# Rows that land last first, and blocks asked for one group ahead, for the unsplit experts of a mixture layer

## The chip, the cores and the metric

The kernel runs on one core of one Trainium2 chip. The metric is the device time of one execution in microseconds (us), lower is better.

## What is computed

The reference runs a small model of two blocks over 256 tokens of width 1024: two hybrid layers (mLSTM and dilated attention), a pooling layer with a dense feed-forward part, and an attention layer with a mixture of experts behind it. The change touches the mixture alone:

```python
def moe_ffn(x, router, w_gu, w_down):
    xt = x.reshape(B * S, D)                       # 256 x 1024
    logits = (xt @ router).astype(jnp.float32)
    top_v, top_i = lax.top_k(logits, TOP_K)        # 2 of 8 experts
    w = jax.nn.softmax(top_v, axis=-1)
    combine = ...                                  # weight of each expert for each token
    for e in range(N_EXPERTS):                     # 8, d_ff 3584
        y = y + combine[:, e:e + 1] * swiglu(xt, w_gu[e], w_down[e])
```

Everything is float32. Each expert has 42 MiB of weights, so all eight are 336 MiB, and each of them is read once.

## The kernel before

The experts are sorted by the number of tokens that chose them, and place 0 has most. Places 0 to 3 are the **split** experts: tiles of 128 token rows (place 0 has a second one of 64). Each MiB of their weights lands in a buffer of the tag `raw` and is split into a high and a low part (`whi` by ScalarE in line 147, `wlo` by VectorE in line 148). A product is then three matmuls of 128x512 (lines 209 to 211), or two for the tile of 64 rows (lines 1304 and 1305). I call these the wide products. Places 4 to 7 are the **unsplit** experts (`full` in the code): tiles of 64 rows (places 4 and 5) or 32 rows (6 and 7). Their products read `raw` as it landed, in plain float32, with 64 or 32 columns of the array, in line 1313. I call these the narrow products. The trace shows each of them as two MATMUL records.

Each expert is worked through in seven steps of 512 hidden units. One step has three **blocks** of 2 MiB: gate (`up1`), up (`up2`) and, two steps later, down (`down`). A block is two DMAs of 1 MiB on SyncE's queue (line 132, `wload`), the first for the rows k = 0 to 3 (0 and 1 for down), the second for the rest. The **group** of a block is all its products for one tile: eight narrow products for an unsplit expert, in the order of k.

`run_experts` is a generator that stops after each group. `moe_layer` runs two of them: places 0 to 3 in the outer loop, and places 6, 7, 4, 5 as `light`, which is moved on by a share of a group for each group of the outer one (`due` grows by 1.5 with place 0, by 0.86 with places 1 to 3). All eight of them share `K.raw`, seven buffers of 1 MiB. A wide block is asked for by `ahead` after the products of the block before it in the same generator. An unsplit block is asked for in `take`, at the head of its own group. A load waits until one of the seven buffers is free, with all later loads queued behind it. A buffer is free when `whi` and `wlo` are made (split), or when the last narrow product has read it (unsplit).

The order of instructions on each engine is made when the kernel is built: a scheduler takes the program's order and its own estimate of the times, and may set other work of the engine between two products of a group when it believes that the second half has not landed. On the chip each engine keeps that order.

Of the kernel before, what the change touches and what calls it, by code (L numbers as in the profile page):

```python
# [18 lines left out]
KT = D // 128  # L19
# [132 lines left out]
def behind(K, hold=None):  # L152

    es = ExitStack()
    for ins in K.hold if hold is None else hold:
        es.enter_context(K.tc.issue_after(ins.ins))
    return es


class Raw:  # L160


    def __init__(self, K, src, kt, n):
        self.per = min(kt, 2048 // n)
        self.parts = [wload(K, src[:, k:k + self.per, :], self.per, n) for k in range(0, kt, self.per)]
# [48 lines left out]
def bank(K, tag):  # L214
    return K.ps.tile([128, 512], F32, name=tag, tag=tag, bufs=K.banks[tag])
# [255 lines left out]
def gate_rows(K, pool, cst, gT, S):  # L471
# [9 lines left out]
    nc.gpsimd.memset(one, 1.0)  # L481
    LI, LF, FC, G, EN, TMP, TMP2, M = range(8)
    R = lambda q: gm if q == M else (ga if q < 4 else gb)[:36, q % 4, :]
# [9 lines left out]
    for d in range(2):  # L493
        s = slice(32 * d, 32 * d + 4)
        v = (lambda a: a[s]) if d == 0 else (lambda a: a[s][:, ::-1])
        nc.vector.tensor_tensor_scan(v(R(FC)), v(one), v(R(LF)), 0.0, op0=OP.mult, op1=OP.add)
    nc.vector.tensor_tensor(R(G), R(LI), R(FC), op=OP.subtract)
    for d in range(2):
        s = slice(32 * d, 32 * d + 4)
        v = (lambda a: a[s]) if d == 0 else (lambda a: a[s][:, ::-1])  # L500
        nc.vector.tensor_tensor_scan(v(R(M)), v(one), v(R(G)), -BIG, op0=OP.mult, op1=OP.max)
    nc.vector.tensor_tensor(R(TMP), R(FC), R(M), op=OP.add)
# [3 lines left out]
    pt = bank(K, "acc")[:, :144].rearrange("p (q t c) -> p q t c", q=2, t=2)  # L506
    for q, src in enumerate((G, EN)):
        for t in range(2):
# [729 lines left out]
def buffer(K, pool, name, i, shape, dt, bufs):  # L1238

    b = K.boxes.get(name)  # L1240
    return b[i % len(b)] if b else pool.tile(shape, dt, name=name, bufs=bufs)
# [17 lines left out]
def gather(K, pool, x, R, cw, p, tl, n):  # L1259

    gather_x(K, pool, x, R, p, tl, n)
    gather_w(K, pool, cw, p, tl, n)
# [37 lines left out]
def prod(K, tl, ps, x, w, start, stop):  # L1300

    nc = K.nc
    if tl.kind == "h":
        nc.tensor.matmul(ps, x[:, 0, :], w[0], start=start, stop=False)
        nc.tensor.matmul(ps, x[:, 0, :], w[1], start=False, stop=stop)
    else:
        mm3(nc, ps, (x[:, 0, :], x[:, 1, :]), w, start, stop)


def prod_full(K, tl, ps, c, x, w, start, stop):  # L1310


    K.nc.tensor.matmul(ps[tl.m * c:tl.m * c + tl.m], x, w, start=start, stop=stop)


def fold(K, pool, a, ps, m=64):

    K.nc.scalar.activation(a, ps[64:128, :], AF.Copy)
    K.nc.vector.tensor_tensor(a, ps[0:64, :], a, op=OP.add)
    if m == 32:  # L1320
        b = pool.tile([32, 512], F32, name="fq")
        K.nc.scalar.activation(b, a[32:64], AF.Copy)
        K.nc.vector.tensor_tensor(a[0:32], a[0:32], b, op=OP.add)
    return a[:m]


class Expert:
    def __init__(self, p, tiles):
        self.p, self.tiles = p, [Tile(*t) for t in tiles]
        self.full = self.tiles[0].full  # L1330


def run_experts(K, pool, A, x, R, ri, cw, y, experts, hook=None, last=False):
# [3 lines left out]
    NF = FE // 512  # L1337

    def begin(E):
        with behind(K, K.line):  # L1340
            e = nc.sync.value_load(ri[0:1, E.p:E.p + 1], min_val=0, max_val=NE - 1)
        gu = A["moe_gu"][ds(e, 1)].rearrange("o c q p (k n) -> (o c) q p k n", k=4)
        E.gu = [Packed(gu[c], 4) for c in range(2 * NF)]
        E.dn = Packed(A["moe_dn"][ds(e, 1)].rearrange("o b p (k n) -> (o b) p k n", k=2), 2)
        for n, tl in enumerate(E.tiles):
            tl.n, tl.g = (f"l{E.p}", "l") if tl.full else (n, n)
        enter(E, 0)

    def enter(E, n):
        if E.tiles[n].xg is None:  # L1350
            gather(K, pool, x, R, cw, E.p, E.tiles[n], E.tiles[n].n)

    def load(kind, E, f):
        B = Raw if E.full else W
        return B(K, E.gu[f + NF * kind], KT, 512) if kind < 2 else B(K, E.dn[:, f * 4:f * 4 + 4, :], 4, 1024)

    def take(kind, E, f):
        got.append((kind, E, f))
        if (kind, E, f) not in blocks:
            blocks[kind, E, f] = load(kind, E, f)  # L1360
        return blocks.pop((kind, E, f))

    def ahead():
# [3 lines left out]
        if n < len(order) and not order[n][1].full:  # L1367
            blocks[order[n]] = load(*order[n])

    def up1(E, f):  # L1370
        w = take(0, E, f)
        for tl in E.tiles:
            ps = bank(K, "mm")
            for k in range(KT):
                if tl.full:
                    G = 128 // tl.m
                    prod_full(K, tl, ps, k % G, tl.xg[:, k], w(k, 0, 512), k < G, k >= KT - G)
                else:
                    prod(K, tl, ps, tl.xg[:, k], w(k, 0, 512), k == 0, k == KT - 1)
            a = buffer(K, pool, f"sg{tl.g}", E.p * NF + f, [128, 512], F32, 2)  # L1380
            nc.scalar.activation(a[:tl.m], fold(K, pool, a[:64], ps, tl.m) if tl.m < 128 else ps, AF.Silu)
            tl.sg[f] = a

    def up2(E, f):
        w = take(1, E, f)
        for tl in E.tiles:
            ps = bank(K, "mm")
            for k in range(KT):
                if tl.full:
                    G = 128 // tl.m  # L1390
                    prod_full(K, tl, ps, k % G, tl.xg[:, k], w(k, 0, 512), k < G, k >= KT - G)
                else:
                    prod(K, tl, ps, tl.xg[:, k], w(k, 0, 512), k == 0, k == KT - 1)
            m = tl.m
            u = ps if m == 128 else fold(K, pool, pool.tile([64, 512], F32, name="fu"), ps, m)
            nc.vector.tensor_tensor(tl.sg[f][:m], u, tl.sg[f][:m], op=OP.mult)
# [17 lines left out]

    def down(E, f):
        w = take(2, E, f)
        for tl in E.tiles:
            if tl.full:
                if f == 0:
                    tl.acc = [bank(K, "acc") for _ in range(2)]  # L1420
                for k in range(4):
                    for h in range(2):
                        if tl.m == 32:
                            prod_full(K, tl, tl.acc[h], 2 * (k % 2) + (h ^ (k // 2)), tl.hT[f][:, k],
                                      w(k, h * 512, (h + 1) * 512), f == 0, f == NF - 1)
                        else:
                            prod_full(K, tl, tl.acc[h], h ^ (k % 2), tl.hT[f][:, k],
                                      w(k, h * 512, (h + 1) * 512), f == 0 and k < 2, f == NF - 1 and k >= 2)
                continue
            if tl.sb:  # L1430
                if f == 0:
                    a = buffer(K, pool, "sacc", 0, [128, D], F32, 1)
                    tl.acc = [a[:, 0:512], a[:, 512:1024]]
                for h in range(2):
                    ps = bank(K, "mm")
                    for k in range(4):
                        prod(K, tl, ps, tl.hT[f][:, k], w(k, h * 512, (h + 1) * 512), k == 0, k == 3)
                    if f == 0:
                        nc.vector.tensor_copy(tl.acc[h], ps)
                    else:  # L1440
                        nc.vector.tensor_tensor(tl.acc[h], ps, tl.acc[h], op=OP.add)
                continue
            if f == 0:
                tl.acc = [bank(K, "acc") for _ in range(2)]
            for k in range(4):
                for h in range(2):
                    prod(K, tl, tl.acc[h], tl.hT[f][:, k], w(k, h * 512, (h + 1) * 512),
                         f == 0 and k == 0, f == NF - 1 and k == 3)
# [35 lines left out]
    def settle():  # L1484
# [3 lines left out]
        if late:  # L1488
# [3 lines left out]
    late, begun, blocks, got = [], set(), {}, []  # L1492
    N = len(steps)
    order = [(kind, *steps[i - (kind == 2) * 2]) for i in range(N + 2) for kind in range(3)
             if (i < N if kind < 2 else i >= 2 and not (last and i == N + 1))]
    for i in range(N + 2):
        for E, f in steps[i:i + 3]:
            if id(E) not in begun:
                begun.add(id(E))
                begin(E)  # L1500
        if i < N:
            E, f = steps[i]
# [15 lines left out]
        if i >= 2:  # L1518
            E, f = steps[i - 2]
# [15 lines left out]
def moe_layer(K, x, A, out, ps1, S):  # L1535
    nc = K.nc
    with ExitStack() as es:
# [6 lines left out]
        with K.tc.tile_pool(name="exp", reuse_waits="tile", bufs=1) as ep:  # L1544
# [15 lines left out]
            for t in range(2):  # L1560
                nc.vector.tensor_scalar(y[:, t, :], x[:, t, :], ALPHA, None, op0=OP.mult)
            go = lambda *a: run_experts(K, ep, A, x, R, ri, cw, y, *a)
            E[0].tiles[1].sb = True
            b = [ep.tile([128, 2048], t, name=f"box{n}") for n, t in enumerate((F32R, F32, F32))]
# [170 lines left out]
```

## Time and profile before

| | us |
|---|---|
| median of three runs | 2013.59 |
| lowest and highest | 2011.82, 2013.74 |
| the profiled execution, its own time | 2013.14 |
| span of its trace | 2011.4 |
| start of the first expert DMA | 1083.3 |
| end of the mixture's products on TensorE | about 1995 |

The profiled execution stands 0.45 us under the median, and 1.7 us lie outside its span. TensorE is busy for 96% of the span. From 1083 us on the mixture's weights stream in, and the DMA engines are as busy as TensorE. An end of a matmul in the trace is modelled, so for TensorE I read the distances from start to start.

### The profile page before, as it was taken

Reading aid. Unit: us, or ns where it says so; the run is one execution under the profiler, and the core shown is the slowest. Engines: PE = TensorE matmul, PEld = TensorE weight load, DVE = VectorE, ACT = ScalarE, POOL = GpSimd, SP = SyncE. Lnnn points to the kernel's source line nnn. Section 1 sums busy time; section 2 is a strip of 40 time slices with the busy share of each in tenths; the row PEclk is TensorE's granted clock in tenths of the full one; section 3 lists DMA queues with packets and bytes.
Section 4 is the critical chain, followed back from the end, with each engine's and each line's share of the span. In section 5 each row is a group of like instructions: output and inputs, shape, how many; then the busy total and the mean of one; then the engine's idle time right before and its main releaser. Section 6 shows DMA issues by size and latency. Waiting matters only on the chain. (4 is left out here: it accounts for less than half of the span.)

```text
span 2011.4 us, 27838 instructions
## 1 busy us (share of the span) xinstructions
PE 1936.6 (96%) x11039; PEld 1492.6 (74%) x11039; DVE 1263.4 (63%) x1721; ACT 960.5 (48%) x1195; POOL 35.2 (2%) x39
## 2 busy tenths in 40 slices
PE   7999999999999899999997999999999999999996
PEld 7879998888999899989776766665556556655563
DVE  6876555877555644466767555666666665656655
ACT  6565444665444444435342544445455544545442
POOL 0000000000000200000000000000000000000000
PEclk9999999999999999999997999999999999999998
DMA  9434555535555365552004789999999999999994
GB/s 341 164 116 160 176 190 179 173 126 171 203 173 205 138 200 186 166 191 85 6 1 180 303 348 391 391 403 380 426 405 413 409 395 422 399 410 384 420 422 168
DMA packets 137851, 523.68 MB, mean 260 GB/s; under 512 B 12016, under 2 KB 44144, under 8 KB 94832
## 3 DMA queue, kind: packets, MB, share of 16 engines
q1 hardware_dynamic: 137568, 521.74, 67.5%
q8 instruction: 89, 1.46, 0.3%
q14 instruction: 50, 0.41, 0.1%
q10 hardware_dynamic: 144, 0.07, 0.0%
HBM read 520.73 MB, written 1.05 MB: 259 GB/s over the span
## 5 line engine op out<-in xcount | busy, mean ns | idle before, releaser
L148 DVE TENSOR_TENSOR wlo<-raw,whi 128x2048 fp32r<-128x2048 f32 (+2 forms) x335 | 716.0, 2155 | 328.8 <-ACT whi L147 321.0
L147 ACT ACTIVATE whi<-raw 128x2048 fp32r<-128x2048 f32 (+2 forms) x337 | 600.3, 1805 | 313.1 <-DMA raw<-in_moe_gu_dram 68.7
L209 PE MATMUL mm<-xT,whi 128*128 128x256 f32 (+1 forms) x824 | 237.1, 288 | 0.8 <-ACT mqk L459 0.4
L211 PE MATMUL mm<-xT,wlo 128*128 128x256 f32 (+1 forms) x824 | 234.4, 284 | 0.0
L210 PE MATMUL mm<-xT,whi 128*128 128x256 f32 (+1 forms) x824 | 233.9, 284 | 0.3
L210 PE MATMUL acc<-wlo,hT 128*128 128x512 f32 x568 | 224.8, 396 | 4.7 <-DVE wlo L148 4.7
L211 PE MATMUL acc<-whi,hT 128*128 128x512 f32 x568 | 221.8, 391 | 0.0
L209 PE MATMUL acc<-whi,hT 128*128 128x512 f32 x568 | 215.7, 393 | 2.7 <-ACT whi L147 2.7
L209 PE MATMUL mm<-whi,xg 128*128 128x512 f32 x448 | 184.1, 411 | 4.8 <-ACT whi L147 1.7
L210 PE MATMUL mm<-wlo,xg 128*128 128x512 f32 x448 | 181.1, 404 | 4.2 <-DVE wlo L148 4.2
L211 PE MATMUL mm<-whi,xg 128*128 128x512 f32 x448 | 178.0, 397 | 0.0
L209 PEld LDWEIGHTS mm<-xT,whi 128*128 128x128 f32 (+1 forms) x824 | 155.8, 189 | 4.6 <-issue 1.1
L210 PEld LDWEIGHTS mm<-xT,whi 128*128 128x128 f32 (+1 forms) x824 | 155.8, 189 | 3.3 <-DVE xT L678 1.1
L211 PEld LDWEIGHTS mm<-xT,wlo 128*128 128x128 f32 (+1 forms) x824 | 155.7, 189 | 0.6
L210 PEld LDWEIGHTS acc<-wlo,hT 128*128 128x128 f32 x568 | 106.7, 188 | 41.2 <-issue 9.1
L209 PEld LDWEIGHTS acc<-whi,hT 128*128 128x128 f32 x568 | 106.0, 188 | 31.0 <-issue 5.8
L211 PEld LDWEIGHTS acc<-whi,hT 128*128 128x128 f32 x568 | 106.7, 188 | 25.1 <-issue 3.3
L209 PEld LDWEIGHTS mm<-whi,xg 128*128 128x128 f32 x448 | 85.7, 191 | 48.2 <-issue 17.1
L210 PE MATMUL mx<-xT,whi 128*128 128x256 f32 x416 | 117.8, 283 | 0.0
L209 PE MATMUL mx<-xT,whi 128*128 128x256 f32 x416 | 117.8, 283 | 0.0
L211 PE MATMUL mx<-xT,wlo 128*128 128x256 f32 x416 | 117.8, 283 | 0.0
L210 PEld LDWEIGHTS mm<-wlo,xg 128*128 128x128 f32 x448 | 86.0, 192 | 37.3 <-issue 11.4
(379 smaller groups left out, 2906.1 us busy)
## 6 DMA issues: line engine op xcount, KB each, us to landing
raw<-in_moe_gu_dram SPq DMA_DIRECT2D x224, 1024.0 KB, 9.0
raw<-in_moe_dn_dram SPq DMA_DIRECT2D x110, 1024.0 KB, 9.1
raw<-in_w_up_dram SPq DMA_DIRECT2D x32, 1024.0 KB, 5.6
raw<-in_w_down_dram SPq DMA_DIRECT2D x32, 1024.0 KB, 5.2
raw<-in_w_in_dram SPq DMA_DIRECT2D x26, 1024.0 KB, 6.1
raw<-in_ffn_w_gu_dram SPq DMA_DIRECT2D x22, 1024.0 KB, 5.0
raw<-in_ffn_w_down_dram SPq DMA_DIRECT2D x11, 1024.0 KB, 4.8
raw<-in_nsa_w_in_dram SPq DMA_DIRECT2D x10, 1024.0 KB, 5.0
```

The lines of the kernel that those rows point to most:

```text
L147: nc.scalar.activation(h, d, AF.Copy)
L148: K.lo.tensor_tensor(l, d, h.bitcast(F32), op=OP.subtract)
L209: nc.tensor.matmul(ps, l[0], r[0], start=start, stop=False)
L210: nc.tensor.matmul(ps, l[0], r[1], start=False, stop=False)
L211: nc.tensor.matmul(ps, l[1], r[0], start=False, stop=stop)
```

## The change

Three things change, all for the unsplit experts. `up_full` takes the rows in the order k = 4 to 7, 0 to 3, and `down` in the order 2, 3, 0, 1: a group begins with the rows of its block's second DMA. `take` asks for the next block in the order of the generator before it returns the present one, if its expert has begun (`E.e`). The blocks, the products and their number are the same.

```diff
@@ take
         if (kind, E, f) not in blocks:
             blocks[kind, E, f] = load(kind, E, f)
+        n = order.index((kind, E, f)) + 1
+        if E.full and n < len(order) and order[n][1].e:
+
+            blocks[order[n]] = load(*order[n])
         return blocks.pop((kind, E, f))
...
+    def up_full(tl, ps, w):
+
+        G = 128 // tl.m
+        for n in range(KT):
+            k = (n + KT // 2) % KT
+            prod_full(K, tl, ps, k % G, tl.xg[:, k], w(k, 0, 512), n < G, n >= KT - G)
@@ up1, and up2 likewise
-            for k in range(KT):
-                if tl.full:
-                    G = 128 // tl.m
-                    prod_full(K, tl, ps, k % G, tl.xg[:, k], w(k, 0, 512), k < G, k >= KT - G)
-                else:
+            if tl.full:
+                up_full(tl, ps, w)
+            else:
+                for k in range(KT):
                     prod(K, tl, ps, tl.xg[:, k], w(k, 0, 512), k == 0, k == KT - 1)
@@ down
-                for k in range(4):
+                for n in range(4):
+                    k = (n + 2) % 4
```

On TensorE, in the middle of place 2's work, this is one gate group of an unsplit expert with 64 rows before the change. `mm_14147` is its bank, `raw_14143` and `raw_14145` are the two MiB of its block, and `mm_14167` is the group of a split expert:

```order
L1313 MATMUL mm_14147<-raw_14143,box2_9664 64x512 x4
L1406 MATMUL mm_14160<-ident_70,sg0_13972 128x128 x4
L209 MATMUL mm_14167<-whi_14133,xg0_12654 128x512
L210 MATMUL mm_14167<-wlo_14134,xg0_12654 128x512
...
L209 MATMUL mm_14167<-whi_14139,xg0_12654 128x512
L1313 MATMUL mm_14147<-raw_14145,box2_9664 64x512 x4
L210 MATMUL mm_14167<-wlo_14140,xg0_12654 128x512
L211 MATMUL mm_14167<-whi_14139,xg0_12654 128x512
```

The same group in the changed program, where `mm_14171` is the split expert's group and `acc_13513` its sum in `down`:

```order
L210 MATMUL mm_14171<-wlo_14144,xg0_12658 128x512
L211 MATMUL mm_14171<-whi_14143,xg0_12658 128x512
L1313 MATMUL mm_14220<-raw_14149,box2_9664 64x512 x4
L1313 MATMUL mm_14220<-raw_14147,box2_9664 64x512 x4
L209 MATMUL acc_13513<-whi_14199,hT0_14014 128x512
```

Before, the two halves stood apart, the second of them inside the other expert's group; now they follow each other, second MiB first, and stand between two groups.

On SyncE's queue, shortly ahead of that place, before the change (`moe_gu` are gate and up, `moe_dn` down; `raw_14044` to `raw_14086` are two blocks of a split expert, `raw_14092` and `raw_14094` a down block of an unsplit one, `raw_14143` its next block):

```order
L132 DMA raw_14044<-in_moe_dn_dram 128x2048
L132 DMA raw_14050<-in_moe_dn_dram 128x2048
L132 DMA raw_14080<-in_moe_gu_dram 128x2048
L132 DMA raw_14086<-in_moe_gu_dram 128x2048
L132 DMA raw_14092<-in_moe_dn_dram 128x2048
L132 DMA raw_14094<-in_moe_dn_dram 128x2048
L132 DMA raw_14131<-in_moe_gu_dram 128x2048
L132 DMA raw_14137<-in_moe_gu_dram 128x2048
L132 DMA raw_14143<-in_moe_gu_dram 128x2048
```

And with it (the unsplit down block is `raw_13997` and `raw_13999`, its next one `raw_14096` and `raw_14098`, and the two split blocks are `raw_14048` to `raw_14090`):

```order
L132 DMA raw_13997<-in_moe_dn_dram 128x2048
L132 DMA raw_13999<-in_moe_dn_dram 128x2048
L132 DMA raw_14048<-in_moe_dn_dram 128x2048
L132 DMA raw_14054<-in_moe_dn_dram 128x2048
L132 DMA raw_14084<-in_moe_gu_dram 128x2048
L132 DMA raw_14090<-in_moe_gu_dram 128x2048
L132 DMA raw_14096<-in_moe_gu_dram 128x2048
L132 DMA raw_14098<-in_moe_gu_dram 128x2048
L132 DMA raw_14135<-in_moe_gu_dram 128x2048
```

The blocks of the unsplit expert each moved ahead of the split blocks that stood in front of them, here two blocks for the first and one for the next.

## Rows read from the trace of the kernel before

**Rows 1.** The page, part 1: engine, busy us (share of span), instructions.

```profile
PE 1936.6 (96%) x11039; PEld 1492.6 (74%) x11039; DVE 1263.4 (63%) x1721; ACT 960.5 (48%) x1195; POOL 35.2 (2%) x39
```

**Rows 2.** Busy time by stretch: us, busy by engine, PEclk, DMA share, GB/s.

```profile
1083.00:1130.00 47.00, 43.60 (x213) 36.91 (x214) 26.90 (x58) 22.54 (x24) 0.00 (x0) 0.79 0.75 294
1130.00:1370.00 240.00, 238.33 (x1302) 159.06 (x1301) 145.62 (x157) 116.54 (x130) 0.00 (x0) 1.00 0.94 382
1370.00:1500.00 130.00, 119.68 (x599) 74.49 (x597) 89.47 (x76) 68.59 (x60) 0.00 (x0) 0.99 0.99 408
1500.00:1960.00 460.00, 456.62 (x2041) 275.09 (x2037) 286.29 (x214) 229.00 (x184) 0.00 (x0) 1.00 0.99 408
1960.00:1997.00 37.00, 32.13 (x136) 17.05 (x134) 19.38 (x24) 12.06 (x14) 0.00 (x0) 1.00 0.57 211
```

**Rows 3.** The same view, 10 us in which the DMA engines never pause.

```profile
1290.00:1300.00 10.00, 10.00 (x56) 6.83 (x55) 6.80 (x6) 4.56 (x6) 0.00 (x0) 1.00 1.01 427
```

**Rows 4.** TensorE's waits, 1370 to 1500: us in total, times, longest.

```profile
PE mm L210 <- DVE wlo L148: 2.3, 2, 1.8
PE acc L209 <- ACT whi L147: 2.1, 1, 2.1
PE acc L210 <- DVE wlo L148: 2.0, 3, 0.9
PE mm L209 <- ACT whi L147: 1.7, 1, 1.7
```

**Rows 5.** The same view, 1500 to 1960.

```profile
PE mm L210 <- DVE wlo L148: 1.9, 3, 0.9
PE acc L210 <- DVE wlo L148: 1.0, 2, 0.5
```

**Rows 6.** Line 1313: what ended the weight loads' idle time (us, times).

```profile
  DMA raw<-in_moe_dn_dram: 0.4, 1
  DMA raw<-in_moe_gu_dram: 0.4, 1
```

**Rows 7.** TensorE in order of time: start, us, instruction; a divided group of 64 rows.

```profile
1743.61 1.89 PE L1313 MATMUL mm<-raw,box 128*64 128x512 f32 x8
...
1748.45 0.39 PE L211 MATMUL mm<-whi,xg 128*128 128x512 f32 x1
1748.67 0.39 PE L209 MATMUL mm<-whi,xg 128*128 128x512 f32 x1
1748.99 1.94 PE L1313 MATMUL mm<-raw,box 128*64 128x512 f32 x8
1750.86 0.51 PE L210 MATMUL mm<-wlo,xg 128*128 128x512 f32 x1
1751.20 0.40 PE L211 MATMUL mm<-whi,xg 128*128 128x512 f32 x1
1751.44 0.40 PE L209 MATMUL mm<-whi,xg 128*128 128x512 f32 x1
```

**Rows 8.** The same view, an undivided group of 64 rows.

```profile
1852.01 3.65 PE L1313 MATMUL mm<-raw,box 128*64 128x512 f32 x16
1855.60 0.50 PE L209 MATMUL mm<-whi,xg 128*128 128x512 f32 x1
```

**Rows 9.** The same view, groups of 32 rows: one undivided, one half.

```profile
1388.86 1.93 PE L1313 MATMUL mm<-raw,xgq 128*32 128x512 f32 x16
1390.71 0.50 PE L209 MATMUL mm<-whi,xg 128*128 128x512 f32 x1
...
1395.48 1.07 PE L1313 MATMUL mm<-raw,xgq 128*32 128x512 f32 x8
1396.47 0.50 PE L211 MATMUL mm<-whi,xg 128*128 128x512 f32 x1
```

**Rows 10.** Waits of SyncE's DMA queue over the span: us, times, longest.

```profile
SPq L132 <- PE mm L1313: 254.1, 76, 13.4
SPq L132 <- DVE wlo L148: 222.7, 102, 6.7
SPq L132 <- PE acc L1313: 153.8, 48, 15.9
```

**Rows 11.** Line 147, 1500 to 1960: its count, and what ended ScalarE's idle time.

```profile
L147 ACT ACTIVATE whi<-raw x96: 1890/1912/1925, 1500.0 to 1948.7; 128x2048 fp32r<-128x2048 f32 x96
  DMA raw<-in_moe_gu_dram: 54.4, 27
```

More of the change, by code (lines that the diff above doesn't have):

```diff
@@ L1330, in __init__ @@
         self.full = self.tiles[0].full
+        self.e = False
 def run_experts(K, pool, A, x, R, ri, cw, y, experts, hook=None, last=False):
@@ L1346, in begin @@
             tl.n, tl.g = (f"l{E.p}", "l") if tl.full else (n, n)
+        E.e = True
         enter(E, 0)
@@ L1387, in up2 @@
             ps = bank(K, "mm")
[L1388 to L1392, printed above, removed]
+            if tl.full:
+                up_full(tl, ps, w)
+            else:
+                for k in range(KT):
                     prod(K, tl, ps, tl.xg[:, k], w(k, 0, 512), k == 0, k == KT - 1)
@@ L1427, in down @@
                             prod_full(K, tl, tl.acc[h], h ^ (k % 2), tl.hT[f][:, k],
-                                      w(k, h * 512, (h + 1) * 512), f == 0 and k < 2, f == NF - 1 and k >= 2)
+                                      w(k, h * 512, (h + 1) * 512), f == 0 and n < 2, f == NF - 1 and n >= 2)
                 continue
```

## The prediction

> **What bounds the kernel now.** I read the page first. TensorE is busy for 96% of the span [rows 1], so the next view is where the other engines come close: the busy time by stretch, from the first expert DMA to the end of the products [rows 2]. There the reader should compare two columns, TensorE's busy time and the GB/s. What the DMA engines can do is told by a stretch in which they never pause: 427 GB/s [rows 3], which is 1.048576 MB / 427 GB/s = 2.45 us for one MiB. With place 0 (1130 to 1370) TensorE is busy for 238.3 of 240 us and the DMA engines move 382 GB/s: TensorE is the bound, and the stream has 240 x (1 - 382/427) = 25 us to spare. From 1370 to 1500 the stream runs at 408 GB/s, and TensorE is idle for 10.3 of 130 us; most of that are waits for `whi` and `wlo` [rows 4]: the stream is the bound. From 1500 to 1960 TensorE is idle for 3.4 of 460 us, and the stream, at 408, has 460 x (1 - 408/427) = 20 us to spare: both are close to full, TensorE a little closer. Before 1083 nothing changes, so the whole effect lies in these 913 us.
>
> The third view is who waits for whom. The narrow products hardly ever wait for their landing: of 1344 records two did, 0.4 us each [rows 6]. In the other direction the queue waits long for them: 254 and 154 us in which the next load stood still until a narrow product had given its buffer back [rows 10].
>
> **What the change does to TensorE's work.** No product is added or taken away; what changes is how often the array goes from wide to narrow products and back. The row in order of time shows the price. A step between two wide products is 0.23 us (1751.20 to 1751.44). The step from a wide to a narrow one is 0.32 (1748.67 to 1748.99), so entering costs 0.09. Half a group of 64 rows takes 1.87 until the next start (1748.99 to 1750.86), and the first wide product behind it takes 0.34 (to 1751.20), so leaving costs 0.11 more [rows 7]. An undivided group takes 3.59 us [rows 8], against 2 x 1.87 = 3.74 for two halves: 0.15 for the cut itself. With 32 rows it is 1.85 against 2 x 0.99: 0.13 [rows 9].
>
> How often each occurs I counted in the order of the two programs. Narrow products stand in 144 runs before, 122 of them halves of a group, and in 82 runs after, none of them a half. Three stretches:
>
> - Place 0, to about 1370: 27 halves become 13 undivided groups more, 13 x 0.13 = 1.8 us; steps out of narrow into wide fall from 24 to 11, 13 x 0.11 = 1.4; steps in from 29 to 19, 10 x 0.09 = 0.9. Together 4.1 us.
> - Places 6 and 7 beside place 1, to about 1500: 16 halves, 8 x 0.13 = 1.0; steps out 13 to 7, 0.7; steps in 17 to 9, 0.7. Together 2.4 us.
> - The rest: 79 halves, nearly all of 64 rows, 39 x 0.15 = 5.9; steps out 50 to 25, 2.7; steps in 58 to 36, 2.0. Together 10.6 us.
>
> That is 17.1 us less work on TensorE. How much of it reaches the end differs by stretch. In the first TensorE is the bound and the stream has 25 us to spare: all 4.1 us. In the second the stream is the bound: nothing. In the third the ends are 0 (the stream can go no faster) and 10.6 (it can: 408 GB/s would have to become 408 x 460/449.4 = 418, under the 427 it reaches). I take two thirds, 7 us, nearer the upper end, since TensorE's 3.4 idle us are fewer than the stream's 20. Gain of this part: 11 us, ends 4 and 17.
>
> The Trainium skill (Perfetto Trace Analysis, "Identifying the Most-Contended Engine") says that matmul busy time is no good measure of how near TensorE is to its limit, and that the busy time of weight loads is one to go by. That is 275 of 460 us, 60%, in the third stretch [rows 2]; by that rule TensorE has room there, the stream alone is the bound, and the first rival below is the outcome. The rows speak against it in this kernel: a narrow weight load is short beside its product, and the wide steps of 0.23 us follow each other without a hole [rows 7].
>
> **What asking ahead does.** Its direct gain is the wait for the landing, at most 0.8 us [rows 6]; I take nothing. The rotation of k alone moves no wait either, as both halves have landed when the group begins; what it does is make the scheduler keep the group in one piece, which is priced above. What asking ahead costs is room. An unsplit block now stands one split block (sometimes two) earlier on SyncE's queue, so of seven buffers up to four can be held by blocks whose products come later, and each split block lands 2 x 2.45 = 4.9 us later against TensorE's need of it. Queued behind a load that waits for a narrow product are the split loads, and for those ScalarE, VectorE and then TensorE wait. The cover is the time that `whi` and `wlo` lie ready before their first product. From 1500 on it is thin: 27 of 96 splits begin at the moment of landing [rows 11], and TensorE waited for a split five times there, 2.9 us [rows 5]. Lower end: the cover holds, 0. Upper end: TensorE waits in all of the 460 us as it did from 1370 to 1500, 2.3 + 2.1 + 2.0 + 1.7 = 8.1 us in 130 [rows 4], which makes 28.7, 25.8 more than now. I take 3 us, twice the present waits, nearer the lower end: while the stream is the slower one, later landing of split blocks only means that unsplit ones landed sooner, and the second halves' buffers come back earlier in undivided groups (3.6 us after a group's start, where it was 7.2 in the divided one, 1743.61 to 1750.86 [rows 7]).
>
> The end of the program is reordered too: the last unsplit blocks come before the last pieces of place 3. From 1960 to 1997 TensorE is idle for 4.9 us [rows 2]; this is the bound both ways, and I take 0.
>
> **Sum.** -4.1 - 7 + 3 = -8 us, against the profiled execution's 2013.1: 2005. The median of the runs is 0.5 us higher, which I leave out.
>
> **The rivals.**
> - *The stream is the bound.* What TensorE saves after 1500 turns into waits for `wlo`, and only place 0's 4.1 us are left, of which asking ahead takes the 3 us above: 2009 to 2013. For it: 408 of 427 GB/s over 590 us, and 27 splits that start on landing. Against it: TensorE's idle time there is 3.4 us, and the stream was held up by narrow products as well [rows 10].
> - *The split blocks come late.* Up to four buffers are tied up, and TensorE waits for `whi` and `wlo` through the third stretch as it does in the second: -4.1 - 10.6 + 25.8 = +11, so 2024, and from 2017 on if half of the saved time is lost too. It decides as soon as the time for which `wlo` lies ready is mostly under the 4.9 us by which landing moves. For it: rows 5 and 11 as told. Against it: both kinds of block share one stream, and its total is unchanged. The Trainium skill (Perfetto Trace Analysis, "Optimization Strategy") says that a gap which repeats on the engine that should be full can mean that there are too few buffers; no run so far shows that pattern after 1500.
> - *All of it is kept.* TensorE's 17 us come through in full and the stream follows: 1996.
>
> **How the numbers follow.** About 0.2% (4 us) is what a measurement of this kernel tells from no change. The forecast of 2005 (2000 to 2009) has 0.55, the full gain of 1996 has 0.10, the stream as the bound (2009 to 2013) 0.18, late split blocks (2017 to 2026) 0.17. So faster 0.65, the same 0.18, slower 0.17. The range leaves out a tenth or less on each side: down to 1995, and up to 2018, where the slower case begins.
>
> **What would show it.** In the changed profile the narrow products should stand in runs of 16 records throughout, the GB/s from 1500 on should rise from 408 towards 418, and TensorE's waits for `whi` and `wlo` there should stay under some 6 us. If those waits are 15 us or more, the second rival has it; if GB/s and TensorE's busy share both stay and TensorE's waits grow by about what was saved, the first. If narrow loads should show long waits for their DMA, then the step that gives asking ahead no value is wrong.

## The result

The changed kernel takes 2038.71 us (median of four runs, 2036.78 to 2039.65) where the kernel before took 2013.66: a ratio of 1.0126, with a 95% interval of 1.0112 to 1.014. It is 25 us slower; 2005 was forecast, and 2018 was the upper end of the range. The profiled execution has a span of 2036.4 us, against 2011.4.

The page, part 1, of the changed kernel: engine, busy us, share of the span, instructions.

```profile
PE 1933.3 (95%) x11039; PEld 1505.4 (74%) x11039; DVE 1264.7 (62%) x1721; ACT 958.3 (47%) x1195; POOL 35.2 (2%) x39
```

The busy time by stretch, for the stretches of [rows 2]; columns as there (us; PE, PEld, DVE, ACT, POOL busy; PEclk; DMA share; GB/s).

```profile
1083.00:1130.00 47.00, 43.35 (x216) 36.55 (x216) 27.33 (x54) 22.59 (x24) 0.00 (x0) 0.80 0.75 304
1130.00:1370.00 240.00, 236.22 (x1311) 160.30 (x1310) 149.10 (x161) 120.78 (x133) 0.00 (x0) 1.00 0.95 390
1370.00:1500.00 130.00, 116.46 (x574) 77.54 (x577) 83.50 (x74) 64.61 (x57) 0.00 (x0) 0.94 0.93 385
1500.00:1960.00 460.00, 431.60 (x1928) 263.76 (x1920) 271.05 (x204) 212.92 (x173) 0.00 (x0) 0.99 0.97 385
```

Up to 1370 nothing is lost: the stream even runs at 390 GB/s where it was 382. From 1370 on both TensorE and the stream are emptier: TensorE idles 13.5 and 28.4 us in the last two stretches (10.3 and 3.4 before), and the stream falls from 408 to 385 GB/s. Neither of them has become the bound; they wait for something between them.

TensorE's waits from 1500 to 1960, the answer to [rows 5] (us in total, times, longest):

```profile
PE mm L210 <- DVE wlo L148: 19.0, 17, 1.8
PE acc L210 <- DVE wlo L148: 7.3, 7, 1.4
PE mm L209 <- ACT whi L147: 2.0, 2, 1.8
```

It waits for the split halves of the weights: 28.3 us here, 2.9 before. The same view from 1130 to 1990, first before the change:

```profile
PE acc L210 <- DVE wlo L148: 4.7, 6, 1.6
PE mm L210 <- DVE wlo L148: 4.2, 5, 1.8
PE acc L209 <- ACT whi L147: 2.7, 2, 2.1
PE mm L209 <- ACT whi L147: 1.7, 1, 1.7
```

And with it:

```profile
PE mm L210 <- DVE wlo L148: 28.6, 25, 1.8
PE acc L210 <- DVE wlo L148: 9.8, 8, 2.5
PE mm L209 <- ACT whi L147: 6.0, 5, 2.5
PE acc L209 <- ACT whi L147: 0.3, 1, 0.3
```

These are 44.7 us against 13.3, so 31.4 more.

Waiting costs a second time. In five stretches of 50 us the granted clock fell (columns as above):

```profile
1350.00:1400.00 50.00, 45.88 (x247) 29.50 (x240) 32.93 (x32) 23.25 (x23) 0.00 (x0) 0.97 0.91 379
1400.00:1450.00 50.00, 46.18 (x237) 30.08 (x236) 35.01 (x34) 26.87 (x26) 0.00 (x0) 0.97 1.01 426
1450.00:1500.00 50.00, 41.87 (x192) 28.01 (x194) 29.94 (x26) 25.52 (x20) 0.00 (x0) 0.90 0.90 365
1550.00:1600.00 50.00, 45.33 (x197) 27.32 (x195) 32.42 (x26) 22.61 (x19) 0.00 (x0) 0.97 0.96 376
1600.00:1650.00 50.00, 47.13 (x200) 29.16 (x200) 28.38 (x22) 23.60 (x19) 0.00 (x0) 0.97 0.94 370
```

That is (0.03 + 0.03 + 0.10 + 0.03 + 0.03) x 50 = 11 us of full clock. In the kernel before, the same five stretches show 1.00 but for this one of 0.97, which is 1.5 us:

```profile
1450.00:1500.00 50.00, 46.04 (x218) 29.05 (x218) 34.56 (x28) 26.39 (x23) 0.00 (x0) 0.97 0.99 405
```

So some 9.5 us more are lost to the clock.

The account: 31.4 us of waits and 9.5 us of clock, less the 17.1 us of work that the prediction saw saved, are +23.8; measured is +25.0 between the spans. The 17.1 is still the prediction's estimate here; the last table of the experiments measures it.

### The profile page after: what moved, and what is told of

The parts are those of the page before. It is cut to its first block, busy times and chain, and to the rows that moved or that the text cites. A ratio compares the mean times of both kernels' runs of the same rounds, so it can differ in the third digit from the quotient of the medians.

```text
span 2036.4 us, 27790 instructions
## 1 busy us (share of the span) xinstructions
PE 1933.3 (95%) x11039; PEld 1505.4 (74%) x11039; DVE 1264.7 (62%) x1721; ACT 958.3 (47%) x1195; POOL 35.2 (2%) x39
## 5 line engine op out<-in xcount | busy, mean ns | idle before, releaser
L210 PEld LDWEIGHTS acc<-wlo,hT 128*128 128x128 f32 x568 | 107.1, 189 | 36.0 <-DVE wlo L148 14.7
```

The lines of the kernel that those rows point to most:

```text
L210: nc.tensor.matmul(ps, l[0], r[1], start=False, stop=False)
```

## Where the split stood: ScalarE's row

The second rival had said that split blocks would land late and TensorE would wait for that. In the trace a landed MiB waits for something else. ScalarE from 1594 to 1611, in order of time (start, us, instruction; in brackets how long the engine was idle before it, and what ended that). Line numbers of the changed kernel are some dozen higher behind `take`: L1417 (transposes) is 1406 before, L1393 (the gate's `sg`) is 1381, L1478 (`ye`) is 1466.

```profile
1594.54 0.60 ACT L1318 ACTIVATE fu<-mm 64x512 f32<-64x512 f32 x1 [4.35 <-PE mm L1313]
1595.60 1.92 ACT L147 ACTIVATE whi<-raw 128x2048 fp32r<-128x2048 f32 x1 [0.47 <-DMA raw<-in_moe_gu_dram]
1604.65 0.60 ACT L224 ACTIVATE hT<-mm 128x512 fp32r<-128x512 f32 x1 [7.13 <-PE mm L1417]
1605.15 5.50 ACT L147 ACTIVATE whi<-raw 128x2048 fp32r<-128x2048 f32 x3
```

And TensorE at the same time:

```profile
1600.08 3.65 PE L1313 MATMUL acc<-raw,hTl 128*64 128x512 f32 x16
1603.67 0.51 PE L209 MATMUL mm<-whi,xg 128*128 128x512 f32 x1
1604.01 0.60 PE L1417 MATMUL mm<-ident,sg 128*128 128x128 f32 x4
...
1607.11 0.49 PE L209 MATMUL mm<-whi,xg 128*128 128x512 f32 x1
1609.43 0.50 PE L210 MATMUL mm<-wlo,xg 128*128 128x512 f32 x1 [1.83 <-DVE wlo L148]
1609.77 0.40 PE L211 MATMUL mm<-whi,xg 128*128 128x512 f32 x1
1610.01 0.56 PE L209 MATMUL mm<-whi,xg 128*128 128x512 f32 x1
1610.37 0.63 PE L210 MATMUL mm<-wlo,xg 128*128 128x512 f32 x1
1610.80 0.63 PE L211 MATMUL mm<-whi,xg 128*128 128x512 f32 x1
```

The first of the three splits at 1605.15 reads a MiB that had landed at 1598.22 (issued at 1592.82, 5.4 us to landing). ScalarE was idle for 7.13 us up to 1604.65, 6.4 of them with this MiB landed, because the next instruction in its order was another: the copy `hT` out of the bank of the transposes (L224), and TensorE does these transposes (L1417) only behind an undivided unsplit group of 3.6 us. Then the split takes 1.9 us on ScalarE and 2.3 on VectorE, TensorE runs out of halves and waits 1.83 us; and from 1610 on its step is 0.43 us (1610.37 to 1610.80) instead of 0.23: the granted clock is 0.50 from 1610.2 to 1613.4, which is 1.2 GHz, the lower of its two levels.

The Trainium skill (Perfetto Trace Analysis, "Tensor Engine Instruction (MATMUL, LD_WEIGHTS)") says that ScalarE and VectorE are strict first in, first out, unlike TensorE's queue. The 6.4 us beside a landed MiB agree.

This is no single case. The view of line 147 from 1500 to 1960, the answer to [rows 11]:

```profile
L147 ACT ACTIVATE whi<-raw x90: 1896/1906/1925, 1504.2 to 1954.8; 128x2048 fp32r<-128x2048 f32 x90
its engine sat idle before it (us, times) until:
  DMA raw<-in_moe_gu_dram: 32.2, 12
  DMA raw<-in_moe_dn_dram: 5.1, 7
```

If the splits waited for late landings, more of them would begin at the moment of landing. Fewer do: 12 gate and up splits, where it was 27. What ScalarE waits for instead are banks (its waits from 1500 to 1960):

```profile
ACT sg L1393 <- PE mm L211: 78.8, 15, 10.7
ACT box L1318 <- PE mm L1313: 52.4, 13, 6.8
ACT fu L1318 <- PE mm L1313: 42.1, 10, 6.5
```

Before, the first of these was 45.6 us and the other two 29.7 and 28.2.

In the order of the programs on ScalarE I then counted the splits that stand behind a copy out of a bank which the program writes *after* them: 8 of 172 before, 45 with the change. The copies `ye` at the end of an expert are left out of this count; with them it is 47 with the change, and 7 instead of 2 in e3, e5 and e10 below.

The blocks do land later against their use, as the rival said. From its landing to its first product (matched in order) a MiB of gate or up lay 21.1 us on average from 1130 to 1370 before and lies 15.5 with the change; from 1500 on it is 11.2 and 9.3. Over the same stretch its split begins 3.8 us after the landing, 2.4 before. So the cover is thinner and the split is later, and the trace alone does not tell which of the two makes TensorE wait.

So there were two theories. **Theory A, ScalarE's order:** asking ahead makes the scheduler set splits behind copies that wait for TensorE. **Theory B, late landing:** the prediction's own, early unsplit blocks hold the seven buffers and split blocks land late.

## The experiments

The kernel before, run beside these, took 2012.3 to 2012.55 (2013.66 beside the change).

| kernel | median us | ratio to before, 95% interval | splits behind a later copy |
|---|---|---|---|
| the change | 2038.7 | 1.0126, 1.0112 to 1.0140 | 45 |
| e1 rotation alone | 2007.2 | 0.9973, 0.9959 to 0.9987 | 1 |
| e2 asking ahead alone | 2061.1 | 1.0232, 1.0209 to 1.0256 | 56 |
| e4 change, unsplit copies held | 2021.8 | 1.0049, 1.0035 to 1.0062 | 29 |
| e3 change, splits first | 2003.9 | 0.9956, 0.9936 to 0.9976 | 2 |
| e5 the same, gate copy too | 1997.4 | 0.9925, 0.9912 to 0.9939 | 2 |
| e6 rotation, splits made late | 2086.9 | 1.0370, 1.0354 to 1.0386 | by construction |
| e7 change, six buffers | 2048.1 | 1.0175, 1.0159 to 1.0190 | 43 |
| e8 before, splits first | 2011.4 | 0.9994, 0.9984 to 1.0004 | 1 |
| e9 rotation, splits first | 2006.8 | 0.9967, 0.9950 to 0.9983 | 0 |
| e10 asking ahead, splits first | 2038.5 | 1.0131, 1.0114 to 1.0148 | 2 |

### The two halves of the change

e1 leaves out asking ahead:

```diff
@@ take
-        n = order.index((kind, E, f)) + 1
-        if E.full and n < len(order) and order[n][1].e:
-
-            blocks[order[n]] = load(*order[n])
```

> The changed kernel without asking ahead: unsplit groups begin with the second MiB, and SyncE's queue has the order of the kernel before. Every group of narrow products is whole in the program, as in the changed kernel. Theory A (ScalarE's order: since blocks are asked for one group ahead, splits that have landed stand on ScalarE behind copies out of banks that wait for TensorE): only 1 split of 172 stands behind the copy of a later group here, against 8 before and 45 in the changed kernel, so TensorE's waits for whi and wlo after 1370 us stay at or under the 16 us of before, and the 17 us of saved work come through for the larger part: 1997 to 2008. Theory B (late landing: unsplit blocks that were asked for early hold the seven buffers): the loads are where they were, so the same, 1997 to 2009. Were undivided groups themselves the harm, it would be 2025 or more.

It measured 2007.2, 5.3 us under the 2012.55 of before that was run beside it. So undivided groups are no harm, and the rotation alone makes them. But the gain is only a third of the 17 us. The waits of TensorE from 1130 to 1990 show the larger part of why:

```profile
PE mm L1313 <- DMA raw<-in_moe_gu_dram: 16.2, 10, 4.2
PE acc L210 <- DVE wlo L148: 3.7, 3, 1.6
```

A rotated group begins with the MiB that lands last, and ten times it was not there. Neither theory had expected that. The clock falls more often too: 11.9 us are lost to it from 1130 us on, where it was 1.7 before.

e2 leaves out the rotation instead (rows from k = 0 on in both places):

```diff
@@ up_full
-            k = (n + KT // 2) % KT
+            k = n
@@ down
-                    k = (n + 2) % 4
+                    k = n
```

> The changed kernel without the rotation: blocks are asked for one group ahead, rows taken from k = 0 on. Narrow products stand in 140 runs, nearly all of them halves as before, and 56 of 172 splits stand on ScalarE behind the copy of a later group. Theory A (ScalarE's order): the waits of the changed kernel or somewhat more, and no saved work: 2045 to 2065. Theory B (late landing): the loads are as early as in the changed kernel, so its waits, without the 17 us of saved work: 2050 to 2060. The two theories do not part here; were it the pair of edits that does the harm and not the asking alone, it would be near 2014.

2061.1: asking ahead is the half that does the harm. Groups stay divided here, so it also pays the work that the rotation saves.

### Same loads, other order on ScalarE

e3 holds two copies behind the splits that the program writes ahead of them; e4 holds the first of the two alone. `K.cut` is the last split, `behind` sets an order of issue and no wait (the lines that set `K.cut` and `K.soon` up are left out).

```diff
@@ wsplit
-            nc.scalar.activation(h, d, AF.Copy)
+            K.cut = [nc.scalar.activation(h, d, AF.Copy)][:K.soon]
@@ fold (e3 and e4)
-    K.nc.scalar.activation(a, ps[64:128, :], AF.Copy)
+    with behind(K, K.cut): K.nc.scalar.activation(a, ps[64:128, :], AF.Copy)
@@ mid (e3)
-                evac_hl(K, h[:, :, 0, :], h[:, :, 1, :], pt)
+                with behind(K, K.cut): evac_hl(K, h[:, :, 0, :], h[:, :, 1, :], pt)
```

> The changed kernel with one thing more: on ScalarE the first copy out of the bank of an unsplit group, and the copy behind the transposes of a split expert, are held behind the splits that the program writes ahead of them. SyncE's queue is the same row for row, TensorE's order nearly so (174 of some 11000 rows differ); 2 of 172 splits stand behind the copy of a later group, where it is 45 in the changed kernel. Theory A (ScalarE's order): TensorE's waits for whi and wlo after 1370 us fall from 42 us to under 15, the clock stays up, and the time to 1996 to 2010. Theory B (late landing): the loads and the buffers are the same, so the waits stay over 30 us and the time within 8 us of 2038.7.

> As the run with the splits first, but only the copies out of the banks of unsplit groups are held behind the splits; 29 of 172 splits still stand behind the copy of a split expert's transposes. Theory A (ScalarE's order): a part of the gain, about a third to a half of the waits gone: 2017 to 2028. Theory B (late landing): within 8 us of 2038.7.

2003.9 and 2021.8. The loads stand in the same order row for row, the buffers are the same, and 35 us are gone: theory B cannot give that. (TensorE's order differs in 174 rows; what these alone are worth was not tried.) In e3 TensorE waits 17.4 us for halves after 1370, a little over the 15 of theory A, and the clock did not stay up: 8.5 us are lost, 11.9 with the change. ScalarE in e3 at the same place of the program:

```profile
1592.40 1.91 ACT L147 ACTIVATE whi<-raw 128x2048 fp32r<-128x2048 f32 x1 [1.29 <-DMA raw<-in_moe_gu_dram]
1594.86 1.92 ACT L147 ACTIVATE whi<-raw 128x2048 fp32r<-128x2048 f32 x1 [0.54 <-DMA raw<-in_moe_gu_dram]
1596.80 0.60 ACT L224 ACTIVATE hT<-mm 128x512 fp32r<-128x512 f32 x1
```

The splits begin as their MiB lands, and `hT` comes behind them and has nothing left to wait for.

e5 also sets the gate's copy `sg` behind the splits of the up block; for that `ahead` is called just ahead of the copy, in place of after it.

```diff
@@ up1
-            a = buffer(K, pool, f"sg{tl.g}", E.p * NF + f, [128, 512], F32, 2)
+            a = buffer(K, pool, f"sg{tl.g}", E.p * NF + f, [128, 512], F32, 2); tl is E.tiles[-1] and ahead()
-            nc.scalar.activation(a[:tl.m], fold(K, pool, a[:64], ps, tl.m) if tl.m < 128 else ps, AF.Silu)
+            with behind(K, K.cut): nc.scalar.activation(a[:tl.m], fold(K, pool, a[:64], ps, tl.m) if tl.m < 128 else ps, AF.Silu)
@@ ahead
-        if n < len(order) and not order[n][1].full:
+        if n < len(order) and not order[n][1].full and order[n] not in blocks:
```

> As the run with the splits first, and the copy out of the gate bank of a split expert (sg) stands behind the splits of its up block too; for that the up block is asked for just ahead of this copy in the program, while SyncE's queue keeps the same order row for row. With the splits first, 8 of the 18 waits for whi and wlo after 1130 us that are longer than 0.35 us had exactly this copy in front of the split. Theory A (ScalarE's order): these waits go, 8 to 10 us with the clock, so 1993 to 2000, the fastest so far. Theory B (late landing): within 4 us of 2003.9.

1997.4, 0.75% under the kernel before and the fastest of all. Line 147 from 1500 to 1960 in e5, and its busy time in that stretch:

```profile
L147 ACT ACTIVATE whi<-raw x96: 1893/1915/1923, 1505.5 to 1950.6; 128x2048 fp32r<-128x2048 f32 x96
its engine sat idle before it (us, times) until:
  DMA raw<-in_moe_gu_dram: 79.2, 43
  DMA raw<-in_moe_dn_dram: 44.4, 27
```

```profile
1500.00:1960.00 460.00, 451.94 (x2057) 284.22 (x2056) 289.02 (x217) 233.74 (x185) 0.00 (x0) 1.00 0.99 414
```

70 of 96 splits begin at landing (19 of 90 with the change), and the stream reaches 414 GB/s. From landing to first product a MiB of gate or up lies only 7.3 us there on average (8.0 in e3, 9.3 with the change), and still TensorE waits least. The split itself begins 0.7 us after the landing there on average, 3.8 with the change: with prompt splits a thinner cover was enough.

For each product of TensorE that came over 0.35 us late and began as its half was ready, I looked up what stood in front of that split on ScalarE. The table adds up how much longer than 0.23 us those steps were, from 1130 on:

| in front of the split | change | e4 | e3 | e5 |
|---|---|---|---|---|
| copy out of an unsplit bank, L1318 | 16.6 | 0 | 0 | 0 |
| copy of the transposes, L224 | 18.2 | 17.7 | 3.0 | 3.0 |
| the gate's copy, L1393 | 7.3 | 8.3 | 8.1 | 1.4 |
| other work, VectorE, the landing | 10.6 | 14.1 | 13.6 | 16.8 |
| sum, us | 52.7 | 40.1 | 24.7 | 21.2 |

Each hold takes away its own row and leaves the other named rows within 1 us; the last row grows, and 7.1 us of it are the copies `ye` in each of e4, e3 and e5. The landing itself stands for 0.5 us of the change's 52.7 and for 2.7 of e5's 21.2. The times follow in the same order: 2038.7, 2021.8, 2003.9, 1997.4. They fall by 41.3 us in all, the table by 31.5; of the rest 6.8 are clock (11.9 us lost with the change, 5.1 in e5).

### The other way round, and the buffers

e6 takes e1, whose loads are those of the kernel before, and spoils ScalarE's order (left out here: the lines of `W` that put a split off, the first value of `K.out`, and those that take asking ahead out as in e1).

```diff
@@ load
-        B = Raw if E.full else W
+        B = Raw if E.full else lambda *z: W(*z, late=kind in (2,) and E.p > 0)
@@ take
-        return blocks.pop((kind, E, f))
+        B = blocks.pop((kind, E, f)); return B if E.full else B.split()
@@ wsplit
-        with behind(K, list(K.hold) + K.hold_at.pop(K.loads - 1, [])):
+        with behind(K, list(K.hold) + K.hold_at.pop(K.loads - 1, []) + K.out):
@@ fold
-    K.nc.scalar.activation(a, ps[64:128, :], AF.Copy)
+    K.out = [K.nc.scalar.activation(a, ps[64:128, :], AF.Copy)]
```

> The rotation alone (2007 us), and the order on ScalarE made bad on purpose: the splits of the down blocks of places 1 to 3, 40 of them, are written in the program where the block is used, and held behind the last copy out of the bank of an unsplit group. SyncE's queue is row for row that of the kernel before. Theory A (ScalarE's order): 20 blocks whose splits, some 4.3 us for the first of them, begin only after a copy that waits for TensorE; 1 to 3 us of waiting each and the clock with it: 2030 to 2075. Theory B (late landing): no load is moved, so within 6 us of 2007.

2086.9, 80 us more than e1 with not a load moved, and over the range of theory A too. That range was for 40 splits; as built, the hold reaches every split that is written behind an unsplit copy, those of place 0 among them. TensorE's longest waits from 1130 to 1990:

```profile
PE acc L209 <- ACT whi L147: 22.7, 11, 2.7
PE acc L210 <- DVE wlo L148: 18.2, 12, 3.1
PE mm L1313 <- DMA raw<-in_moe_gu_dram: 10.6, 4, 4.0
```

So it shows the direction; its size is not that of the 40.

e7 is the change with six buffers (`bufs=6` in the pool `raw`), e8 the kernel before with the holds of e5.

> The changed kernel with six buffers for raw instead of seven; 43 of 172 splits stand behind the copy of a later group, where it is 45. Theory A (ScalarE's order): the buffers are not what holds the splits up, so little is added: 2038 to 2050. Theory B (late landing): each split block lands one MiB or more (2.45 us) later once again, so the waits grow by as much as the change brought: 2055 to 2075.

> The kernel before with the same holds on ScalarE as the run with the gate copy too: the number of splits behind the copy of a later group falls from 8 to 1, groups stay divided, loads stay where they are. Theory A (ScalarE's order): at most the 12 waits of before that stood behind ScalarE go, some 15 us of them, of which the stream between 1370 and 1500 keeps the larger part: 2003 to 2012. Theory B (late landing): 2012 to 2014.

e7 takes 2048.1, some 9 us more than the change: a buffer is worth something, but far less than the change cost. There 42 of 91 splits begin at landing from 1500 on (19 of 90 with seven buffers), so loads do come late with six. The Trainium skill (Perfetto Trace Analysis, "Optimization Strategy") says that a repeating gap on the engine that should be full can mean too few buffers. The gap was here, and the seven buffers were not its main cause: e3 closed most of it with the same seven.

e8 takes 2011.4, no difference. Its waits for halves from 1130 to 1990 fall from 13.3 to 8.4 us, but other waits and the clock take that up. The kernel before had next to nothing to gain on ScalarE; the fault came with asking ahead.

### What each half is worth once the order is right

e9 is e1 and e10 is e2, both with the holds of e5.

> The rotation without asking ahead, with the same holds on ScalarE as the run with the gate copy too (1997 us): what asking ahead is worth once ScalarE's order is right. With the rotation alone TensorE waited 16.2 us, ten times, for the landing of an unsplit block, and that kernel had only 1 of 172 splits behind a later copy. Theory A (ScalarE's order was the only harm of asking ahead, and asking ahead takes away the waits for landing that the rotation brings): those 16 us stay here, so 2002 to 2009. If asking ahead has no worth of its own: 1995 to 1999.

> Asking ahead without the rotation, with the same holds: 2 of 172 splits behind a later copy, groups divided as before (137 runs of narrow products). What the whole groups are worth. Theory A: the waits go as in the run with the gate copy too, from 2061 us, but the 17 us of work for divided groups stay: 1997 + 17 = 2014, 2009 to 2018. Theory B (late landing): the loads are those of the changed kernel, so it stays over 2040.

e9 takes 2006.8, as e1 does, and still waits for the landing of unsplit blocks. So asking ahead is worth 2006.8 - 1997.4 = 9.4 us beside the rotation. TensorE's waits in e9 from 1130 to 1990:

```profile
PE mm L1313 <- DMA raw<-in_moe_gu_dram: 17.5, 11, 4.1
```

e10 takes 2038.5, where I had expected 2014; by the number alone it stands next to the "over 2040" of theory B. The same view of it:

```profile
PE mm L210 <- DVE wlo L148: 12.9, 10, 1.8
PE acc L210 <- DVE wlo L148: 8.0, 9, 2.5
PE mm L209 <- ACT whi L147: 6.8, 5, 3.2
```

27.7 us of waits for halves are left (43.2 in e2, 18.1 in e5). None of its 24 late products goes back to a landing. In 9 of them `wlo` began over 1 us after `whi` was done, behind the product of gate and up (L1407) on VectorE, an engine on which I hold nothing; their steps are 9.4 us over the usual ones. Another 17.4 us stand on ScalarE behind two copies that no hold reaches, `fq` of the experts with 32 rows (L1322, 8.1) and `ye` (L1478, 9.3). So it is again what stands ahead of the split on its engine, and not late landing.

To see what whole groups are worth I divided TensorE's time from 1130 us to the start of its last product: waits for halves, all other waits of the view, what the clock took by the granted clock of the trace, and the rest, which I call work (waits too short for the view are in it).

| us | waits for halves | other waits | clock | work |
|---|---|---|---|---|
| before | 13.3 | 5.4 | 1.7 | 844.7 |
| the change | 44.7 | 2.3 | 11.9 | 831.0 |
| e1 | 5.8 | 23.5 | 11.9 | 820.7 |
| e5 | 18.1 | 2.4 | 5.1 | 823.6 |
| e10 | 27.6 | 7.1 | 10.2 | 845.4 |

Where groups are divided (before, e10) the work is 845 us, where they are whole it is 821 to 831. From e10 to e5, which have the same loads and holds, it falls by 21.8 us, with 9.5 less of waits for halves, 4.7 of other waits and 5.1 of clock: together the 41. Without the rotation, asking ahead costs time even with ScalarE's splits first.

## Why the prediction was wrong

- **The bound, and the work saved: right.** TensorE goes to and fro less often, and an undivided group takes 3.59 us as in [rows 8] (1600.08 to 1603.67). The saving of 17.1 us is there, if anything too small: TensorE's work falls by 13.7 us with the change, where short waits hide in it, and by 21.1 in e5. e5, with the change's own loads, is 14.9 us under its 2012.3 of before, although its waits for halves are 18.1 us against 13.3. That its 1997.4 stands so near the 1996 of the rival in which all is kept is partly luck: more work was saved than that rival had, and waits and clock took some of it. (One slip of that sum: its upper end of 17 counts 2.4 us of a stretch that the text sets at nothing; without them it is 14.7.)
- **"The rotation of k alone moves no wait": wrong.** I took it from [rows 6], where narrow products hardly waited for a landing. But there the scheduler had set other work between the halves, and that was what hid the second landing. The rotation took the cover away: 16.2 us in e1.
- **"Its direct gain is the wait for the landing, I take nothing": wrong by the same step.** The cover being gone, asking ahead is worth 9.4 us (e9 to e5).
- **The cost of asking ahead, 3 us between 0 and 25.8: wrong in mechanism and in size. This is the step that failed.** The prediction let only later landing cost something, by buffers held too long. It measured 31.4 us of waits and some 9.5 of clock, and the wait was for the splits' place in ScalarE's order: with that order mended and every load in its place, 41 us came back (e5). I had followed the change to SyncE and TensorE, where I laid the two orders side by side, and not to ScalarE and VectorE, which stand between them. And the upper end was made of waits alone; that TensorE's clock falls behind them was left out, though [rows 2] show 0.99 in the one stretch where it waited.
- **[rows 11] were read the wrong way.** That 27 of 96 splits began at the moment of landing I took as thin cover. It says only that ScalarE stood ready. With the down blocks it was 34 of 96; with 19 of 90 the kernel is slow, with 70 of 96 it is fastest. But the count alone does not rank kernels: e7 and e10 have 42 of 91 and 42 of 92, and are slow.
- **The second rival named the right wait and the right sign, and the wrong cause.** Its 2024 was 15 us short, and its lower end of 2017 has the wrong sign: if half of the saved time is lost too, 2024 rises to some 2031. The blocks did land later against their use, by 5.6 us with place 0 and 1.9 from 1500 on, near the 4.9 that it had worked out; but in e5 they lie shorter still, without the harm. Its test in the prediction, waits of 15 us or more, came out as it said, with 28; by that test alone late landing would have passed as shown. Only e3, with every load in its place, told the two apart.

Why the scheduler sets splits behind those copies only with asking ahead was not tried. Its order follows its own estimate of when a MiB lands; the trace shows that for 31 of the 39 late products of the change the MiB had been there for 4.8 us or longer when its split began.

## What to carry to other kernels

When a change moves loads, lay the order of every engine between the load and its last reader side by side, not only the queue's and the bound engine's: one instruction that waits in the middle, on an in-order engine, holds all that have landed behind it. A wait that the profile doesn't show may be hidden by the very arrangement that the change removes. And where a test in the profile fits two causes, keep one experiment that holds the first fixed (here the queue, row for row) and moves the second alone.

## Not expected of the hardware

A wait of under 2 us can stand ahead of a fall of TensorE's clock: after the one of 1.83 us that ended at 1609.43 the granted clock is 0.50 from 1610.2 on (step 0.43 us, where it is 0.23). With the change the clock took some 9.5 us beside 31.4 us of waiting. That is no fixed share. From 1650 to 1700 TensorE idles 4.7 us and the granted clock stays at 1.00, while from 1600 to 1650 it idles 2.9 us at 0.97. And in the table above e1 loses as much clock as the change, 11.9 us, with 29.3 us of waits where the change has 47.0.
